# Modulation sums of a two-layer encoder moved from matmuls against c to elementwise work on GpSimd and VectorE

## The chip, the cores and the metric

The kernel runs on one core of a Trainium2 chip. The metric is device microseconds of one execution (median of several); lower is better. Engine names in the rows: PE is TensorE's matmul, PEld its weight load, DVE is VectorE, ACT is ScalarE, POOL is GpSimd, SP is the engine that issues most DMAs.

## What is computed

The reference runs DEPTH = 2 layers on x of 256 x 1024, everything in fp32:

```
c_act = silu(c)                                   # 1024 values
for l in range(2):
    mod = c_act @ w_ada[l] + b_ada[l]             # 1024 x 3072 matrix: shift, scale, gate
    shift, scale, gate = split(mod, 3)
    h = rms_norm(x, pre_norm_g[l]) * (1 + scale) + shift
    proj = h @ w_in[l]                            # 1024 x 4096
    att = dilated_attention(q, k, v, rel_bias) * silu(g_att)
    cnv = b_gate * short_conv(c_gate * u, conv_w[l]) * silu(g_conv)
    x = x + gate * rms_norm(concat(att, cnv) @ w_out[l], post_norm_g[l])
```

The change is about `c_act @ w_ada[l]`: a single row times 12 MB of weights for each layer. "Modulation sums" are these 3072 sums over 1024 inputs.

## The kernel before

All weights stream from HBM once, mostly in pieces of 1 MB (128 partitions x 8 KB) into six `raw` buffers of the pool `wp`. The main products are made in three passes of a split precision: each raw piece is split into a part `hi` (a cast on ScalarE, L145) and a part `lo` (raw minus hi on VectorE, L146), six buffers each, and `mm3` (L237 to L239) adds hi·hi, hi·lo and lo·hi.

The work has these stages, with the times of the profiled execution. A written-out prologue (to about 56 us) does layer 0's projections q, k, v and g row by row of w_in, together with the first two thirds of layer 0's modulation sums. Then comes layer 0's main stage (56 to 158 us): the remaining input projections in *chunks* of 256 columns (`chunk`, 48 matmuls each), the attention heads (`attend`), and three of the four steps of the output projection. After each chunk `side()` is called: it starts the heads and the side tasks listed for this step and lets each running side task go on to its next `yield`. A written-out transition (158 to 183 us) finishes the output projection, adds the residual, normalizes x again and makes layer 1's values. Layer 1's main stage (183 to 300 us) is like that of layer 0, and the output closes it. In the main stages the order on each engine is settled at compile time by a scheduler which takes the program's order as priority; each engine then runs its own list in order.

In the main stages the modulation sums are side tasks. Layer 0's stage has two gate tasks for its own gate and four `mods_task`s for layer 1's shift and scale (12 MB of w_ada in all), layer 1's has one gate task; each takes two pieces of 1024 x 256. Half of layer 1's gate is loaded at the end of layer 0 and summed in the transition (`add_sums(g_ps, gw, ...)`). A task yields twice and then emits its load and its sums. There are two ways to sum: `sums` has TensorE do it all, with silu(c) in 32 equal columns as the stationary operand (L295: 16 matmuls of 256 columns, four at a time in the four 32-row strips of the result); `vector_sums` multiplies and adds over the eight inputs of a partition on VectorE in two chains (L279, L281) and leaves four matmuls with a block of ones (L287). In layer 0 gate 0 and `mods_task(2)` go by `vector_sums`, the other four by `sums`; layer 1's gate task goes by `vector_sums`. An fp32 matmul shows as two instructions in the profile.

ScalarE copies each result from PSUM (L300). For shift and scale a GpSimd DMA packs it into a tile `parts`, which is transposed (L575) and finished by small VectorE operations in the transition (L578, L579, L268 to L270). For the gate, `gate_rows` adds two halves by a matmul with `pair` (L323), adds and multiplies b_ada and post_g on one row (L327, L328), writes the row to DRAM and reads it back to all partitions as `gg` (L330, L333).

Of the kernel before, what the change touches and what calls it, by code (L numbers as in the profile page):

```python
# [31 lines left out]
WC = 256  # L32
GATE_AT = ((0, 3), (None, 1))
ROWS_AT = (6, 5)
MODS_AT = (1, 2, 4, 5)
# [33 lines left out]
def encoder_kernel(ctx, tc, x, c, w_ada, b_ada, pre_g, w_in, conv_w, rel_bias, w_out, post_g, rows, out):  # L69
    nc = tc.nc  # L70
# [39 lines left out]
    ones = const.tile([P, 32], F32, name="ones")  # L110
# [86 lines left out]
    last_rstd = [None]  # L197
# [52 lines left out]
    def ada_load(l, k0, n):  # L250

        if n > 1:
            return [load_ada(l, base + k0 * P, n * P) for base in (0, D)]
        raw = wp.tile([P, 2, KC, n * P], F32, name="raw")
        for t in range(2):
            nc.sync.dma_start(raw[:, t], w_ada[l].rearrange("(k p) n -> p k n", p=P)[:, :, t * D + k0 * P:t * D + (k0 + n) * P])  # L256
        return [raw[:, t] for t in range(2)]

    def set_mods(l, k0, cols):

        n = cols.shape[-1]
        A, B = [m[:, k0:k0 + n] for m in mods[l]]
        if n == 1:
            shift, gain = vt[:, 8 + 24 * l + k0:9 + 24 * l + k0], vt[:, 56 + 8 * l + k0:57 + 8 * l + k0]
            nc.vector.tensor_scalar(A, cols[:, 1], scale1[:, l, k0:k0 + 1], gain, op0=ALU.add, op1=ALU.mult)
            nc.vector.tensor_scalar_add(B, cols[:, 0], shift)
            return
        nc.vector.tensor_add(A, cols[:, 1], scale1[:, l, k0:k0 + n])  # L268
        nc.vector.tensor_mul(A, A, vt[:, 56 + 8 * l + k0:56 + 8 * l + k0 + n])
        nc.vector.tensor_add(B, cols[:, 0], vt[:, 8 + 24 * l + k0:8 + 24 * l + k0 + n])  # L270

    def vector_sums(raws, pool, tag):

        for kk in range(KC // 2):
            for kh in range(2):
                k = kk + kh * (KC // 2)
                for raw in raws:
                    if kk == 0:
                        nc.vector.tensor_scalar_mul(raw[:, k], raw[:, k], c_rep[:, k, 0:1])  # L279
                    else:  # L280
                        nc.vector.scalar_tensor_tensor(raw[:, k], raw[:, k], c_rep[:, k, 0:1], raw[:, k - 1],  # L281
                                                       op0=ALU.mult, op1=ALU.add)
        g_ps = pool.tile([P, raws[0].shape[-1]], F32, name=tag)
        for kh in range(2):
            for t in range(2):
                j = 2 * kh + t
                nc.tensor.matmul(g_ps[32 * j:32 * j + 32, :], ones, raws[t][:, (kh + 1) * (KC // 2) - 1, :], start=True, stop=True)  # L287
        return take_sums(g_ps)
# [9 lines left out]
    def take_sums(g_ps, copy=nc.scalar.copy):  # L298
        acc = work.tile(list(g_ps.shape), F32, name="acc", bufs=5)
        copy(acc, g_ps)  # L300
        return acc
# [15 lines left out]
    gg = {}  # L317

    def gate_rows(l, accs):

        row_ps = pm.tile([2, 2, WC], F32, name="pm")
        for q in range(2):
            nc.tensor.matmul(row_ps[:, q], pair, accs[q], start=True, stop=True)  # L323
        b_row, g_row = [work.tile([2, 2, WC], F32, name=n, tag="junk", bufs=3) for n in ("b_row", "g_row")]
        nc.gpsimd.dma_start(b_row, b_ada[l, 2 * D:3 * D].rearrange("(h q n) -> h q n", h=2, q=2))
        nc.gpsimd.dma_start(g_row, post_g[l].rearrange("(h q n) -> h q n", h=2, q=2))
        nc.vector.tensor_add(b_row, row_ps, b_row)  # L327
        nc.vector.tensor_mul(b_row, b_row, g_row)  # L328
        r_dr = dram.tile([2, 2, WC], F32, name=f"r_dr{l}")
        nc.gpsimd.dma_start(r_dr, b_row)  # L330
        gg[l] = const.tile([P, 2, 512], F32, name="gg")
        src = r_dr[:]
        nc.gpsimd.dma_start(gg[l], bass.AP(tensor=src.tensor, offset=src.offset, ap=[[0, P], [1, D]]))  # L333

    def load_gate(l, q):
        return [load_ada(l, 2 * D + (q + 2 * h) * WC, WC) for h in range(2)]

    gate_acc = {}
# [34 lines left out]
    for l in range(DEPTH):  # L373
# [187 lines left out]

        if nxt:
            parts = const.tile([32, P], F32, name="parts")

        def mods_task(s):
            yield
            yield
            acc = (vector_sums if s == 2 else sums)(ada_load(l + 1, 2 * s, 2), pm, "pm")
            nc.gpsimd.dma_start(parts[8 * s:8 * s + 8], acc[0:P:32].rearrange("j (b p) -> j b p", p=P))
            if s < 3:  # L570
                return
            yield
            yield
            col_ps = pm.tile([P, 4, 2, 2, 2], F32, name="pm")
            nc.tensor.transpose(col_ps.rearrange("p s h t b -> p (s h t b)"), parts, ident[:32, :32])  # L575
            cols = small.tile([P, 2, KC], F32, name="cols", bufs=1)
            half = small.tile([P, 4, 2, 2], F32, name="half", bufs=1)
            nc.vector.tensor_copy(half, col_ps[:, :, 0])  # L578
            nc.vector.tensor_add(cols.rearrange("p t (s b) -> p s t b", b=2), col_ps[:, :, 1], half)  # L579
            set_mods(l + 1, 0, cols)  # L580

        def gate_task(q):
            yield
            yield
            gate_acc.setdefault(l, []).append((vector_sums if q == l else sums)(load_gate(l, q), pm, "pm"))

        def rows_task():
            with tc.issue_after(last_rstd[0].ins):
                gate_rows(l, gate_acc[l])
            yield  # L590
# [11 lines left out]
        for q, at in enumerate(GATE_AT[l]):  # L602
            if at is not None:
                starts[at].append(gate_task(q))
        starts[ROWS_AT[l]].append(rows_task())
        if nxt:
            for q, at in enumerate(MODS_AT):
                starts[at].append(mods_task(q))
# [99 lines left out]
        if nxt:  # L708
            vw_raw = [load_raw(l + 1, 2 * AW + i * WC) for i in range(2)]
            gw = load_gate(l + 1, 0)  # L710
# [46 lines left out]
        with tc.manual_schedule(engines=MANUAL):  # L757
# [40 lines left out]
            g_ps = pm.tile([P, WC], F32, name="pm")  # L798
            add_sums(g_ps, gw, range(2))
# [3 lines left out]
            add_sums(g_ps, gw, range(2, 4))  # L803
            gate_acc[l + 1] = [take_sums(g_ps)]
# [25 lines left out]
```

## Time and profile before

| | us |
|---|---|
| median of 3 runs | 310.91 (310.74 to 310.98) |
| profiled execution, its own time | 311.03 |
| its span (first to last instruction) | 309.3 |
| busy: PE, DVE, ACT, POOL | 300.4, 211.8, 178.1, 24.1 |

The span is what the views below cover; the profiled execution has 1.7 us around it. A matmul's row is as long as its passage through the array, and the next one starts before it ends, so a busy TensorE is judged by the distance of the starts. The granted TensorE clock is 1.00 of full speed in every stretch up to 300 us.

### The profile page before, as it was taken

Reading aid. Unit: us, or ns where it says so; the run is one execution under the profiler, and the core shown is the slowest. Engines: PE = TensorE matmul, PEld = TensorE weight load, DVE = VectorE, ACT = ScalarE, POOL = GpSimd, SP = SyncE. Lnnn points to the kernel's source line nnn. Section 1 sums busy time; section 2 is a strip of 40 time slices with the busy share of each in tenths; the row PEclk is TensorE's granted clock in tenths of the full one; section 3 lists DMA queues with packets and bytes.
Section 4 is the critical chain, followed back from the end, with each engine's and each line's share of the span. In section 5 each row is a group of like instructions: output and inputs, shape, how many; then the busy total and the mean of one; then the engine's idle time right before and its main releaser. Section 6 shows DMA issues by size and latency. Waiting matters only on the chain.

```text
span 309.3 us, 6050 instructions
## 1 busy us (share of the span) xinstructions
PE 300.4 (97%) x2421; PEld 261.3 (84%) x2421; DVE 211.8 (68%) x430; ACT 178.1 (58%) x318; POOL 24.1 (8%) x49
## 2 busy tenths in 40 slices
PE   8999999999999999999999999999999999999991
PEld 6878998899877779878677899999998989998881
DVE  3554446589988498688449798798868686845333
ACT  4633445599247243989437584569637695663211
POOL 5220000000000000110013410000000001000011
PEclk9999999999999999999999999999999999999998
DMA  7999999999979999989912399758548632000002
GB/s 244 327 350 330 322 351 343 358 350 348 313 248 344 348 348 323 404 281 351 345 65 66 114 350 344 227 153 242 152 135 272 265 137 70 0 2 0 2 35 102
DMA packets 65692, 72.39 MB, mean 234 GB/s; under 512 B 1778, under 2 KB 61526, under 8 KB 65664
## 3 DMA queue, kind: packets, MB, share of 16 engines
q1 hardware_dynamic: 64512, 70.39, 70.9%
q0 software_dynamic: 784, 1.20, 1.2%
q8 instruction: 19, 0.31, 0.4%
q10 hardware_dynamic: 368, 0.42, 0.4%
q14 instruction: 9, 0.07, 0.1%
HBM read 70.91 MB, written 1.07 MB: 233 GB/s over the span
## 4 chain that ended last, share of the span: by engine, by line
PE 83%; DVE 4%; SPq 4%; DMA 3%; POOL 1%; issue 1%; ACT 1%; POOLq 0%; DVEq 0%; ACTq 0%
PE pm L237 21%; PE pm L238 21%; PE pm L239 21%; PE ps L554 4%; DMA raw<-in_w_in 3%; PE pm L295 3%; PE ps L546 3%; SPq L394 2%; PE ps L295 2%; SPq L256 2%; PE ps L238 2%; PE ps L237 2%; PE ps L239 1%; PE ps L528 1%; PE ps L529 1%
## 5 line engine op out<-in xcount | busy, mean ns | idle before, releaser
L237 PE MATMUL pm<-hT_hi,hi 128*128 128x256 f32 x408 | 116.2, 285 | 0.0
L238 PE MATMUL pm<-hT_lo,hi 128*128 128x256 f32 x408 | 114.9, 282 | 0.1
L239 PE MATMUL pm<-hT_hi,lo 128*128 128x256 f32 x408 | 114.4, 280 | 0.0
L146 DVE TENSOR_TENSOR lo<-raw,hi 128x1024 fp32r<-128x1024 f32 (+1 forms) x94 | 94.0, 1028 | 29.6 <-ACT hi L145 29.2
L145 ACT CAST hi<-raw 128x1024 fp32r<-128x1024 f32 (+1 forms) x94 | 80.5, 893 | 32.9 <-PE pm L238 15.3
L237 PEld LDWEIGHTS pm<-hT_hi,hi 128*128 128x128 f32 x408 | 76.8, 188 | 5.6 <-issue 4.5
L238 PEld LDWEIGHTS pm<-hT_lo,hi 128*128 128x128 f32 x408 | 76.8, 188 | 2.5 <-issue 1.9
L239 PEld LDWEIGHTS pm<-hT_hi,lo 128*128 128x128 f32 x408 | 76.8, 188 | 1.2 <-issue 0.8
L237 PE MATMUL pm<-hi,hT_hi 128*128 128x512 f32 (+1 forms) x68 | 23.7, 348 | 0.0
L239 PE MATMUL pm<-hi,hT_lo 128*128 128x512 f32 (+1 forms) x68 | 23.6, 346 | 0.0
L238 PE MATMUL pm<-lo,hT_hi 128*128 128x512 f32 (+1 forms) x68 | 23.3, 343 | 0.0
L537 ACT ACTIVATE prob<-prob,mx 128x256 f32<-128x256 f32 x32 | 16.0, 503 | 4.0 <-DVE mx L534 3.9
L281 DVE SCALAR_TENSOR_TENSOR raw<-raw,c_rep 128x256 f32<-128x256 f32 x36 | 16.0, 477 | 0.1
L182 ACT ACTIVATE junk<-pm 128x512 f32<-128x512 f32 (+1 forms) x9 | 5.0, 550 | 17.2 <-PE pm L239 17.1
L239 PEld LDWEIGHTS pm<-hi,hT_lo 128*128 128x128 f32 x68 | 12.8, 188 | 2.2 <-DVE hT_lo L231 0.6
L237 PEld LDWEIGHTS pm<-hi,hT_hi 128*128 128x128 f32 x68 | 12.8, 188 | 2.0 <-DVE hT_hi L230 0.4
L724 DVE TENSOR_TENSOR og<-pm,gg 128x512 f32<-128x512 f32 (+1 forms) x9 | 5.6, 630 | 12.7 <-ACT junk L182 12.7
L238 PEld LDWEIGHTS pm<-lo,hT_hi 128*128 128x128 f32 x68 | 12.8, 188 | 1.3
L554 PE MATMUL ps<-pT,v_sb 128*64 128x256 f32 x64 | 13.8, 398 | 0.0
L238 PE MATMUL pm<-lo,mix_a 128*128 128x512 f32 (+1 forms) x36 | 13.4, 373 | 0.0
L237 PE MATMUL pm<-hi,mix_a 128*128 128x512 f32 (+1 forms) x36 | 13.4, 372 | 0.0
L239 PE MATMUL pm<-hi,mix_a 128*128 128x512 f32 (+1 forms) x36 | 12.7, 371 | 0.0
(176 smaller groups left out, 446.0 us busy)
## 6 DMA issues: line engine op xcount, KB each, us to landing
raw<-in_w_in SPq DMA_DIRECT2D x25, 1024.0 KB, 7.6
raw<-in_w_ada SPq DMA_DIRECT2D x16, 1024.0 KB, 10.8
raw<-in_w_ada SPq DMA_DIRECT2D x16, 512.0 KB, 8.4
raw<-in_w_out SPq DMA_DIRECT2D x8, 1024.0 KB, 6.9
raw<-in_w_in SPq DMA_DIRECT2D x7, 896.0 KB, 10.0
u<-t_dr SPq DMA_DIRECT2D x1, 1536.0 KB, 10.0
x_sb<-in_x SPq DMA_DIRECT2D x2, 512.0 KB, 4.3
gg<-r_dr POOLq DMA_DIRECT2D x2, 512.0 KB, 4.2
```

The costliest lines, as they stand in the source:

```text
L145: nc.scalar.copy(hi, raw)
L146: nc.vector.tensor_sub(lo, raw, hi.bitcast(F32))
L237: nc.tensor.matmul(o, ah, bh, start=first, stop=False, **kw)
L238: nc.tensor.matmul(o, ah, bl, start=False, stop=False, **kw)
L239: return nc.tensor.matmul(o, al, bh, start=False, stop=last, **kw)
L256: nc.sync.dma_start(raw[:, t], w_ada[l].rearrange("(k p) n -> p k n", p=P)[:, :, t * D + k0 * P:t * D + (k0 + n) * P])
L281: nc.vector.scalar_tensor_tensor(raw[:, k], raw[:, k], c_rep[:, k, 0:1], raw[:, k - 1], op0=ALU.mult, op1=ALU.add)
L295: nc.tensor.matmul(g_ps[32 * j:32 * j + 32, :], c_rep[:, kk + kh * (KC // 2), :], raws[t][:, kk + kh * (KC // 2), :], start=kk == 0, stop= ...
L394: row_dma[0] = nc.sync.dma_start(raw[:, a:b], w_in[0, k * P:(k + 1) * P, a:b])
L537: nc.scalar.activation(pr_sb[:, t, :], pr_sb[:, t, :], AF.Exp, scale=-1.0, bias=mx[:, t:t + 1], accum_out=sm[:, t:t + 1])
L546: turned[h] = nc.tensor.transpose(t_ps[:, kt, t * P:(t + 1) * P], pr_sb[:, t, kt * P:(kt + 1) * P], ident)
L554: taken[h] = nc.tensor.matmul(a_ps[(hh % 2) * HD:(hh % 2 + 1) * HD, :], qkv["v"][:, kt, hh * HD:(hh + 1) * HD], pT[hh][:, kt, :], start=kt ...
```

## The change

Every piece of 256 columns of w_ada in a main stage becomes a task of its own, given in `PIECES` by the step at which it starts, the engine and the number of yields: in layer 0 seven pieces on GpSimd ("P", four yields) and five on VectorE ("D", one yield), in layer 1 four on GpSimd. The engine multiplies by silu(c) and adds over the eight inputs of each partition: VectorE with one multiplication and seven chained multiply-adds, GpSimd with eight multiplications of 256 columns and three additions of 1024, 512 and 256 columns. After the yields TensorE adds over partitions: for a gate piece one matmul with a 128 x 128 block of ones, which leaves the sums in all partitions; for a shift or scale piece two matmuls whose moving operand is one column of ones. VectorE adds and multiplies the vectors straight from PSUM. `gate_tiles` loads b_ada and post_g broadcast to all partitions by two ScalarE-queue DMAs of 512 KB per layer. The sums in the transition, the `parts` tile, the copies on ScalarE and the trip of the gate through DRAM are gone; all of layer 1's gate is loaded in layer 1. The prologue's sums stay.

```diff
-GATE_AT = ((0, 3), (None, 1))
-ROWS_AT = (6, 5)
-MODS_AT = (1, 2, 4, 5)
+PIECES = (((0, "P", 4), (1, "P", 4), (1, "D", 1), (2, "P", 4),
+           (3, "D", 1), (4, "P", 4), (5, "P", 4), (5, "D", 1), (6, "P", 4), (7, "D", 1), (8, "P", 4), (9, "D", 1)),
+          ((0, "P", 4), (2, "P", 4), (4, "P", 4), (6, "P", 4)))
...
-    ones = const.tile([P, 32], F32, name="ones")
+    ones = const.tile([P, P], F32, name="ones")
...
-    def vector_sums(raws, pool, tag):
...
+    def scaled(raw, on):
+
+        if on == "D":
+            nc.vector.tensor_scalar_mul(raw[:, 0], raw[:, 0], c_rep[:, 0, 0:1])
+            for k in range(1, KC):
+                nc.vector.scalar_tensor_tensor(raw[:, k], raw[:, k], c_rep[:, k, 0:1], raw[:, k - 1],
+                                               op0=ALU.mult, op1=ALU.add)
+            return raw[:, KC - 1]
+        for k in range(KC):
+            nc.gpsimd.tensor_scalar(raw[:, k], raw[:, k], c_rep[:, k, 0:1], 1.0, op0=ALU.mult, op1=ALU.mult)
+        for n in (4, 2, 1):
+            nc.gpsimd.tensor_add(raw[:, 0:n], raw[:, 0:n], raw[:, n:2 * n])
+        return raw[:, 0]
...
-        acc = work.tile(list(g_ps.shape), F32, name="acc", bufs=5)
+        acc = work.tile(list(g_ps.shape), F32, name="acc", bufs=2)
...
-    def gate_rows(l, accs):
...
+    def gate_tiles(l):
+
+        gg[l] = const.tile([P, D], F32, name="gg")
+        gate_b[l] = const.tile([P, D], F32, name="gate_b")
+        for to, src in ((gg[l], post_g[l]), (gate_b[l], b_ada[l, 2 * D:3 * D])):
+            nc.scalar.dma_start(to, bass.AP(tensor=src.tensor, offset=src.offset, ap=[[0, P], [1, D]]))
+
+    def gate_piece(l, i, acc):
+
+        cs = slice(i * WC, (i + 1) * WC)
+        g_ps = pm.tile([P, WC], F32, name="pm")
+        nc.tensor.matmul(g_ps, ones, acc, start=True, stop=True)
+        nc.vector.tensor_add(gate_b[l][:, cs], g_ps, gate_b[l][:, cs])
+        nc.vector.tensor_mul(gg[l][:, cs], gg[l][:, cs], gate_b[l][:, cs])
+
+    def mods_piece(l, i, acc):
+
+        col_ps = pm.tile([P, 2], F32, name="pm")
+        for b in range(2):
+            nc.tensor.matmul(col_ps[:, b:b + 1], acc[:, b * P:(b + 1) * P], ones[:, 0:1], start=b == 0, stop=True,
+                             skip_group_check=True)
+        k0 = 2 * (i % 4)
+        ks = slice(k0, k0 + 2)
+        A, B = mods[l]
+        if i < 4:
+            nc.vector.tensor_add(B[:, ks], col_ps, vt[:, 8 + 24 * l + k0:10 + 24 * l + k0])
+        else:
+            nc.vector.tensor_add(A[:, ks], col_ps, scale1[:, l, ks])
+            nc.vector.tensor_mul(A[:, ks], A[:, ks], vt[:, 56 + 8 * l + k0:58 + 8 * l + k0])
...
-        def mods_task(s):
...
-        def gate_task(q):
...
-        def rows_task():
...
+        def piece_task(i, on, steps):
+            c0 = 2 * D + i * WC if i < 4 else (i - 4) * WC
+            acc = scaled(load_ada(l if i < 4 else l + 1, c0, WC), on)
+            for _ in range(steps):
+                yield
+            if i < 4:
+                gate_piece(l, i, acc)
+            else:
+                mods_piece(l + 1, i - 4, acc)
...
+        gate_tiles(l)
+        for i, (at, on, steps) in enumerate(PIECES[l]):
+            starts[at].append(piece_task(i, on, steps))
...
-            gw = load_gate(l + 1, 0)
...
-            g_ps = pm.tile([P, WC], F32, name="pm")
-            add_sums(g_ps, gw, range(2))
...
-            add_sums(g_ps, gw, range(2, 4))
-            gate_acc[l + 1] = [take_sums(g_ps)]
```

## Rows read from the trace of the kernel before

**Rows 1.** Page, first part: busy time, share of the span, instructions.

```profile
PE 300.4 (97%) x2421; PEld 261.3 (84%) x2421; DVE 211.8 (68%) x430; ACT 178.1 (58%) x318; POOL 24.1 (8%) x49
```

**Rows 2.** Windows by stage: us, busy us of PE, PEld, DVE, ACT, POOL; clock, DMA share, GB/s.

```profile
56.00:158.00 102.00, 102.00 (x807) 85.11 (x799) 77.79 (x159) 65.05 (x114) 3.85 (x6) 1.00 1.00 329
158.00:183.00 25.00, 24.34 (x172) 19.96 (x172) 20.90 (x41) 16.47 (x36) 8.60 (x14) 1.00 0.42 128
183.00:300.00 117.00, 117.00 (x898) 107.76 (x898) 81.65 (x146) 69.94 (x112) 2.15 (x5) 1.00 0.43 140
```

**Rows 3.** Timeline of PE in a plain chunk: start, us, line.

```profile
190.10 0.28 PE L239 MATMUL pm<-hT_hi,lo 128*128 128x256 f32 x1
190.22 0.28 PE L237 MATMUL pm<-hT_hi,hi 128*128 128x256 f32 x1
```

**Rows 4.** Waits of PE, the only one in the transition: us, times, longest.

```profile
PE ps L749 <- DVE xhat L786: 0.6, 1, 0.6
```

**Rows 5.** Chain by line, first 56 to 158 us, then 158 to 184 us.

```profile
by line: PE pm L237 22.7%; PE pm L239 21.3%; PE pm L238 21.0%; PE pm L295 9.4%; PE ps L554 6.2%; PE ps L546 4.0%; PE ps L238 2.7%; PE ps L237 2.7%; PE ps L239 2.7%; PE pm L287 2.2%; PE ps L528 2.1%; PE ps L529 1.9%; PE pm L323 0.8%; PE ps L
...
by line: PE pm L239 12.8%; PE pm L238 9.6%; PE pm L237 9.4%; issue 9.4%; DVE x_sb L729 8.5%; POOL rstd L213 8.1%; DVE hT_lo L231 6.5%; DVE junk L208 5.1%; DVE lo L146 4.7%; DVE og L724 4.6%; DVE vw_q_odd L146 4.4%; PE ps L749 4.1%; DVE hT_h
```

**Rows 6.** Chain in order of time: start, us on the chain, line.

```profile
102.44 1.85 PE pm L295 x28
...
234.78 0.57 PE pm L287 x8
...
250.51 0.95 PE pm L323 x4
```

**Rows 7.** Timeline of PE at a matmul of few columns.

```profile
57.03 0.28 PE L314 MATMUL ps<-pair,acc 128*128 128x2 f32 x2
57.17 0.36 PE L237 MATMUL pm<-hT_hi,hi 128*128 128x256 f32 x1
57.37 0.28 PE L238 MATMUL pm<-hT_lo,hi 128*128 128x256 f32 x1
```

**Rows 8.** Lines of DVE, 56 to 158 us: busy us, mean ns.

```profile
L146 DVE TENSOR_TENSOR lo<-raw,hi 128x1024 fp32r<-128x1024 f32 x26 | 31.1, 1221 | 4.1 <-ACT hi L145 4.1
L281 DVE SCALAR_TENSOR_TENSOR raw<-raw,c_rep 128x256 f32<-128x256 f32 x24 | 10.6, 478 | 0.1
...
L279 DVE TENSOR_SCALAR raw<-raw,c_rep 128x256 f32<-128x256 f32 x8 | 2.4, 348 | 0.0
...
L540 DVE RECIPROCAL rc<-sm 128x2 f32<-128x2 f32 x8 | 1.3, 163 | 2.3 <-ACT prob L537 2.2
...
L231 DVE TENSOR_TENSOR hT_lo<-h,hT_hi 128x256 fp32r<-128x256 f32 x1 | 0.4, 426 | 0.0
```

**Rows 9.** Timelines of POOL and DVE where the two engines meet.

```profile
160.06 0.57 POOL L194 TENSOR_TENSOR rstd<-me,neg_half 128x1 f32<-128x1 f32 x1
...
163.24 1.54 POOL L213 TENSOR_TENSOR rstd<-me,neg_half 128x1 f32<-128x1 f32 x1
...
163.15 1.23 DVE L146 TENSOR_TENSOR lo<-raw,hi 128x1024 fp32r<-128x1024 f32 x1
...
176.77 1.99 POOL L349 MEMSET k_low<- 64x1024 f32 x2 [0.66 <-PE ps L749]
...
177.21 0.67 DVE L230 CAST hT_hi<-h 128x256 fp32r<-128x256 f32 x1 [0.57 <-ACT h L226]
...
179.41 0.29 DVE L230 CAST hT_hi<-h 128x256 fp32r<-128x256 f32 x1
```

**Rows 10.** Lines of POOL by shape: busy us, mean ns.

```profile
L349 POOL MEMSET k_low<- 64x1024 f32 x4 | 3.8, 959 | 6.4 <-PE pm L387 5.6 <-PE ps L749 0.7
...
L86 POOL TENSOR_SCALAR_AFFINE_SELECT ident<-ident 128x128 f32<-128x128 f32 x1 | 0.3, 300 | 0.1
...
L191 POOL TENSOR_TENSOR me<-me,ms 128x1 f32<-128x1 f32 x1 | 0.2, 190 | 0.5 <-ACT junk L182 0.5
```

**Rows 11.** Timeline of SP's DMA issues: a pair of w_ada pieces, layer 0.

```profile
83.47 5.59 SPq L174 DMA_DIRECT2D raw<-in_w_ada  x2
```

More of the change, by code (lines that the diff above doesn't have):

```diff
@@ L250, in ada_load @@
     def ada_load(l, k0, n):
-        if n > 1:
-            return [load_ada(l, base + k0 * P, n * P) for base in (0, D)]
         raw = wp.tile([P, 2, KC, n * P], F32, name="raw")
@@ L259, in set_mods @@
     def set_mods(l, k0, cols):
[L261 to L268, printed above, removed]
@@ L269, in set_mods @@
-        nc.vector.tensor_mul(A, A, vt[:, 56 + 8 * l + k0:56 + 8 * l + k0 + n])
-        nc.vector.tensor_add(B, cols[:, 0], vt[:, 8 + 24 * l + k0:8 + 24 * l + k0 + n])
-    def vector_sums(raws, pool, tag):
[L274 to L288, printed above, removed]
+        A, B = [m[:, k0:k0 + 1] for m in mods[l]]
@@ new lines, in set_mods @@
+        shift, gain = vt[:, 8 + 24 * l + k0:9 + 24 * l + k0], vt[:, 56 + 8 * l + k0:57 + 8 * l + k0]
+        nc.vector.tensor_scalar(A, cols[:, 1], scale1[:, l, k0:k0 + 1], gain, op0=ALU.add, op1=ALU.mult)
+        nc.vector.tensor_scalar_add(B, cols[:, 0], shift)
+    def scaled(raw, on):
[10 more added lines that the diff above has]
+        return raw[:, 0]
@@ L315, in columns @@
         return col_ps
-    gg = {}
-    def gate_rows(l, accs):
[L321 to L333, printed above, removed]
@@ L335, in load_gate @@
-    def load_gate(l, q):
-        return [load_ada(l, 2 * D + (q + 2 * h) * WC, WC) for h in range(2)]
-    gate_acc = {}
+    gg, gate_b = {}, {}
+    def gate_tiles(l):
[9 more added lines that the diff above has]
+        nc.vector.tensor_mul(gg[l][:, cs], gg[l][:, cs], gate_b[l][:, cs])
@@ L558, in encoder_kernel @@
         nxt = l + 1 < DEPTH
-        if nxt:
-            parts = const.tile([32, P], F32, name="parts")
-        def mods_task(s):
[L566 to L580, printed above, removed]
-        def gate_task(q):
-            yield
-            yield
-            gate_acc.setdefault(l, []).append((vector_sums if q == l else sums)(load_gate(l, q), pm, "pm"))
-        def rows_task():
-            with tc.issue_after(last_rstd[0].ins):
-                gate_rows(l, gate_acc[l])
-            yield
+        def piece_task(i, on, steps):
[7 more added lines that the diff above has]
+                mods_piece(l + 1, i - 4, acc)
         o0 = 4 * AW
@@ L601, in encoder_kernel @@
         heads = [[h for h in range(NH) if HEAD_AT[l][h] == i] for i in range(16)]
[L602 to L608, printed above, removed]
+        gate_tiles(l)
+        for i, (at, on, steps) in enumerate(PIECES[l]):
+            starts[at].append(piece_task(i, on, steps))
         running = []
@@ L723, in gated @@
             half, at = cs.start // 512, slice(cs.start % 512, (cs.stop - 1) % 512 + 1)
-            nc.vector.tensor_mul(og[t][half][:, at], o_ps[t][n], gg[l][:, half, at])
+            nc.vector.tensor_mul(og[t][half][:, at], o_ps[t][n], gg[l][:, cs])
         def residual(t, cols=(0, 512, 1024)):
```

## The prediction

> **What bounds the kernel now.** I read the page first: TensorE is busy for 97% of the span [rows 1]. Since busy matmuls may still be slow ones, I then asked for the windows by stage [rows 2] and for the distance of the starts. Both main stages show TensorE busy from end to end, and in a plain chunk a matmul of 256 columns starts every 0.12 us [rows 3]; the list of waits names a single one on TensorE in the transition, 0.6 us [rows 4]. So in the main stages every matmul taken off shortens the stage, provided its feeders keep up. The chain by line says the same for 56 to 158 us: matmul lines and nothing else of weight. From 158 to 184 us it is mixed, with VectorE and GpSimd in front [rows 5]: the transition waits for the normalized x, not for TensorE.
>
> The reader should see two more things in [rows 2]. In layer 0's stage VectorE is busy for 77.8 of 102 us and the DMA engines all the time at 329 GB/s; in layer 1's stage they have 35 us and more than half of the time free. GpSimd is idle nearly throughout. If the change has a price, it is paid in layer 0.
>
> **TensorE's part.** The chain of layer 0's stage gives L295 9.4%, L287 2.2% and L323 0.8% of 102 us [rows 5]: 9.6 + 2.2 + 0.8 = 12.6 us, all removed. Added are four gate matmuls with a full block of ones: the chain has two full fp32 matmuls of 256 columns at L323 for 0.95 us [rows 6], so 0.48 each, 1.9 us. Eight shift and scale pieces make two matmuls of one column each. The nearest row is L314: its matmul takes 0.14 us to the next start, and the one behind it 0.20 in place of 0.12 [rows 7]; a pair costs 0.14 + 0.14 + 0.08 = 0.36, eight 2.9 us. Layer 0 saves 12.6 - 4.8 = 7.8 us. In layer 1, 0.57 + 0.95 go [rows 6] and four gate matmuls, 1.9, come: 0.4 us more.
>
> In the transition 32 instructions of sums go. They fill time in which TensorE waits for x anyway, and behind the second half it waits already [rows 4]: nothing. The small operations that finish shift and scale (five of about 0.17, by the 128x2 row of [rows 8]) leave VectorE, which is on this chain: at most 0.8, I take 0.4 us. TensorE's sum, if everything arrives in time: -7.8 + 0.4 - 0.4 = -7.8 us.
>
> **VectorE's part, layer 0.** The 32 operations of `vector_sums` go: 10.6 + 2.4 = 13.0 us busy [rows 8], and two row operations of about 0.7. A D piece is one L279 and seven L281 at the same means (2.4/8 and 10.6/24): 0.30 + 7 x 0.44 = 3.4 us, five 17.0. Four gate pieces add two operations of 256 columns (0.43 each by L231 [rows 8]): 3.4. Twelve narrow ones at 0.17: 2.0. Net 77.8 - 14.4 + 22.4 = 85.8 us, in a stage which TensorE would end after 102 - 7.8 = 94.2. That fits, with 8 us left. In layer 1 VectorE loses 7 and gains 3.4 us where 35 are idle: nothing.
>
> **GpSimd's part.** No row shows a wide multiplication on it. Its 128x128 select takes 0.30 and a one-column operation 0.19 us [rows 10]: 0.87 ns a column, so about 0.41 us for 256 columns. The memset of 64x1024, 0.96 us, has the same slope. An addition reads two operands: between the one-operand slope and twice that, the three together take 2.1 to 3.7 us. A piece: 8 x 0.41 + 2.1 to 3.7 = 5.4 to 7.0 us; of this 3.3 to 4.9 is streaming (1,792 + 2,048 columns, without the 0.19 that each of 11 instructions costs anyway). Seven pieces are 38 to 49 us of an engine that has about 98 free. A piece has four steps, some 30 us, before TensorE wants it.
>
> The trace speaks against this being free. A reciprocal root of one column takes 0.57 us, but 1.54 when it meets a `lo` subtraction on VectorE: it ends 0.40 us after the subtraction [rows 9]. In turn a cast on VectorE takes 0.67 in place of 0.29 us when GpSimd's memset runs [rows 9]. So each of the two engines can hold the other for an instruction. The Trainium skill, "SBUF — State Buffer", § Who interferes with whom, states it as an exclusive lock on a shared pair of ports, taken by VectorE operations with two SBUF inputs or in a two-port mode and by GpSimd, for the whole instruction; the rows agree as far as they go, and no row shows a wide GpSimd read holding a subtraction. By that rule alone, with whole instructions, the change would cost time: this is the first rival.
>
> What of VectorE is exposed? Of the 77.8 us the operations with two SBUF inputs, and the scalings and casts from SBUF, make 61 (thirteen rows of this view, from L146 with 31.1 to L231 with 0.4 [rows 8]). Less 13.0, plus 17.0, plus 2.4 of the added ones: 67 us by busy time; followed from start to start an L281 takes 0.40 and not 0.48 us, so 63 is nearer. Together with GpSimd: 63 + 23 to 34 (streaming only) = 86 to 97 us, or 63 + 38 to 49 (whole instructions) = 101 to 112. The delayed root ran 0.17 of its 0.57 us before it was held, and the delayed cast needed only a part of its 0.29 behind the memset, so an instruction's fixed part overlaps and the streaming time is the better price. I take its middle, 28: 91 us, just inside the 94.2, and allow 3 us for the places where a late VectorE operation stops TensorE in its fixed order (softmax scaling before the transposes above all). The lead of three chunks of `hi` and `lo` covers the rest.
>
> **Loads.** Before, a pair of pieces is issued at 83.5 [rows 11] and summed from 102.4 us [rows 6]: two buffers for about 22 us, six times. Now a P piece holds one for four steps of 8 us and the landing before them, about 40, seven times, a D piece about 18, five times: 370 against 264 buffer-us, one of the six buffers more on average. Traffic in the stage changes by -2 MB (layer 1's gate) - 0.5 + 1.0 MB. I price this at 0; it shows in a rival. ScalarE loses six copies and gains two DMA issues in this stage, and GpSimd's queue loses its small DMAs: nothing, ScalarE being busy for 65 of 102 us [rows 2].
>
> **Sum.** -7.8 + 3 = -4.8 us. The profiled execution took 311.0 us (span 309.3 and 1.7 around it), 0.1 above the median: I forecast 306 us.
>
> **Rivals.**
> - *The two engines hold each other for whole instructions.* Place: layer 0's stage. For it: [rows 9]; against: the fixed parts overlapped there, and layer 1 has room. It decides from the point at which 63 us and seven pieces exceed 102: 5.6 us per piece. At 7.0 the stage is 112 us and the kernel 10 us slower; in the middle of 5.6 and 7.0 it is 5, and TensorE's stops of 1 to 3 us add to either: 317 us. A page puts the additions at the upper end: the Trainium skill, "GPSIMD Engine Reference", § Performance versus the Vector engine, has 4,497 ns for an addition of 2,048 columns; an estimate from it is 3.9 us for the three, near the 3.7 above, and no run here shows it.
> - *No change.* The freed time is eaten by the stage's other limits: VectorE with GpSimd reaches 102 us, or the DMA engines, always busy now, deliver the stage's loads no faster. 310.5 us.
> - *TensorE waits for pieces or weights.* Its list is fixed; a piece that GpSimd finishes late, or a chunk which found no `raw` buffer, stops everything behind. For it: one buffer less where SP already waits for releases; against: 30 us of time for 7 us of work. One wait of about 1 us per P piece of layer 0 and one missed load of 5 us would turn -4.8 into +7: 313 to 318, I take 314 us.
>
> **Chances and range.** Forecast 0.52 (its own range 302.5 to 309.5: the lower end is the whole of TensorE's 7.8 us and half a microsecond more, the upper end VectorE's delays at twice what I allow), first rival 0.27, no change 0.12, late pieces 0.09. A difference of 0.2%, 0.6 us, is about what a measurement of this kernel can tell. Faster: 0.52 and a third of "no change", 0.56; same 0.08; slower 0.36. The range must take in most of the first rival: 303 to 319 us; about 0.05 lies below it and 0.12 above.
>
> **What would show it.** Right: L295 gone after 60 us; layer 0's stage about 97 us long; GpSimd rows of 0.4 us for 256 columns and under 2 us for 1,024; no wait of TensorE above 1 us in the main stages. `lo` subtractions longer than 1.22 us with GpSimd rows beside them, and waits of TensorE for VectorE, show the first rival; waits for `raw` of GpSimd or for casts, the last. The prediction fails if a GpSimd piece takes over 6 us of VectorE's way, or if TensorE's new matmuls cost more than 0.5 us each.

## The result and the profile after

The changed kernel takes 333.21 us (median of 4 runs, 332.32 to 335.02) against 310.83 (310.55 to 310.98) before: a ratio of 1.0729, interval 1.0683 to 1.0774, 22.4 us slower. The forecast was 306, its range 303 to 319. The profiled execution took 332.32 us, its span is 330.6. The stages below are read from the two profiled executions, whose spans differ by 21.3 us.

Page of the kernel after, first part, and the windows by stage (columns as in [rows 2]):

```profile
PE 299.9 (91%) x2276; PEld 267.6 (81%) x2276; DVE 247.8 (75%) x441; ACT 175.6 (53%) x310; POOL 144.1 (44%) x158
```

```profile
65.05:178.72 113.67, 96.87 (x654) 85.40 (x653) 106.44 (x177) 59.24 (x101) 76.38 (x77) 0.92 0.76 243
178.72:204.00 25.28, 23.12 (x140) 19.52 (x139) 20.34 (x36) 16.56 (x35) 8.22 (x13) 1.00 0.78 252
204.00:321.00 117.00, 116.63 (x893) 108.36 (x892) 84.63 (x132) 69.45 (x111) 51.08 (x47) 1.00 0.45 145
```

I cut both kernels at the same events (the ScalarE activation that ends the prologue, the first square of the output projection, the last transposes of the transition). The prologue went from 61.6 to 65.0 us, layer 0's main stage from 95.9 to 113.7, the transition from 18.1 to 18.0, the rest from 133.7 to 133.9. So the whole loss lies in layer 0's stage (17.8) and the prologue (3.4). The stage before, by the same events:

```profile
61.62:157.56 95.94, 95.94 (x761) 79.87 (x761) 74.52 (x151) 60.60 (x106) 3.85 (x6) 1.00 1.00 329
```

TensorE has 145 instructions fewer on the page, yet its busy time is the same as in [rows 1]; VectorE has 36 us more. In layer 0's stage VectorE is busy for 106 of 114 us and the granted TensorE clock is 0.92. Layer 1's stage holds 51 us of GpSimd work and is not longer: VectorE, busy for 85 of 117 us, has room there.

The chain by line of 65 to 179 us, and TensorE's longest waits in the whole execution (the second is in the prologue):

```profile
by line: DVE lo L148 23.0%; DVE raw L271 13.9%; DMA raw<-in_w_in 11.5%; DVE prob L541 8.5%; issue 7.9%; DVE y L609 4.7%; ACT hi L147 4.6%; DVE raw L269 2.8%; DVE prob L533 2.4%; DVE pT L547 1.6%; ACT k_hh L368 1.5%; DVE gg L322 1.4%; DVE hT
```

```profile
PE pm L241 <- DVE lo L148: 9.5, 3, 6.4
PE ps L285 <- DMA raw<-in_w_ada: 3.3, 2, 2.7
PE ps L545 <- DVE prob L541: 3.0, 4, 2.1
PE pm L239 <- ACT hi L147: 2.3, 2, 1.6
```

In [rows 5] this chain was TensorE's; now VectorE leads it. Its lines in the same stretch, and GpSimd's:

```profile
L148 DVE TENSOR_TENSOR lo<-raw,hi 128x1024 fp32r<-128x1024 f32 x26 | 34.7, 1357 | 5.4 <-ACT hi L147 5.4
L271 DVE SCALAR_TENSOR_TENSOR raw<-raw,c_rep 128x256 f32<-128x256 f32 x35 | 23.5, 673 | 0.4
L541 DVE TENSOR_SCALAR prob<-prob,rc 128x256 f32<-128x256 f32 x16 | 11.1, 735 | 0.0
L533 DVE CUSTOM_DVE_ANT_0 prob<-ps,u 128x256 f32<-128x256 f32 x16 | 6.1, 416 | 0.1
```

```profile
L275 POOL TENSOR_SCALAR raw<-raw,c_rep 128x256 f32<-128x256 f32 x56 | 42.5, 776 | 63.6 <-DMA raw<-in_w_ada 43.0 <-DVE pT L547 13.1 <-PE pm L240 7.5
L277 POOL TENSOR_TENSOR raw<-raw 128x1024 f32<-128x1024 f32 x7 | 18.8, 2685 | 0.4
L277 POOL TENSOR_TENSOR raw<-raw 128x512 f32<-128x512 f32 x7 | 10.1, 1439 | 0.5
L277 POOL TENSOR_TENSOR raw<-raw 128x256 f32<-128x256 f32 x7 | 5.3, 757 | 0.4
```

The same VectorE instructions took 1,221 and 478 ns before [rows 8]. The kernel before's softmax scaling, and its operation that is L533 after:

```profile
L542 DVE TENSOR_SCALAR prob<-prob,rc 128x256 f32<-128x256 f32 x16 | 4.9, 347 | 0.1
L534 DVE CUSTOM_DVE_ANT_0 prob<-ps,u 128x256 f32<-128x256 f32 x16 | 6.1, 420 | 0.3
```

The operations that became longer take their inputs from SBUF; L533, one of whose inputs is in PSUM, keeps its time. One stop in full, from the timelines of VectorE, GpSimd and TensorE:

```profile
81.85 4.84 DVE L271 SCALAR_TENSOR_TENSOR raw<-raw,c_rep 128x256 f32<-128x256 f32 x3
...
87.84 1.41 DVE L148 TENSOR_TENSOR lo<-raw,hi 128x1024 fp32r<-128x1024 f32 x1
...
81.75 4.65 POOL L277 TENSOR_TENSOR raw<-raw 128x256 f32<-128x256 f32 x3
...
82.66 0.28 PE L240 MATMUL pm<-hT_lo,hi 128*128 128x256 f32 x1
89.30 0.58 PE L241 MATMUL pm<-hT_hi,lo 128*128 128x256 f32 x1 [6.37 <-DVE lo L148]
89.68 0.42 PE L239 MATMUL pm<-hT_hi,hi 128*128 128x256 f32 x1
89.90 0.42 PE L240 MATMUL pm<-hT_lo,hi 128*128 128x256 f32 x1
90.11 0.41 PE L241 MATMUL pm<-hT_hi,lo 128*128 128x256 f32 x1
```

Three VectorE steps of a D piece, 0.48 us each when alone, take 4.84 us beside three GpSimd additions (the shape shown is the first one's). The second of each, by itself:

```profile
82.47 2.53 POOL L277 TENSOR_TENSOR raw<-raw 128x1024 f32<-128x1024 f32 x1
...
82.84 2.45 DVE L271 SCALAR_TENSOR_TENSOR raw<-raw,c_rep 128x256 f32<-128x256 f32 x1
```

The addition ends at 85.00 and the VectorE step at 85.29 us. The other two steps also end 0.28 us behind the addition that they met. So VectorE was held to the end of each of these GpSimd instructions. The `lo` behind them comes late and TensorE stands for 6.4 us. Then its matmuls start every 0.21 us in place of the 0.12 of [rows 3]. The windows of two us (columns as in [rows 2]) show why:

```profile
82.00:84.00 2.00, 0.93 (x9) 0.73 (x7) 1.96 (x2) 0.18 (x1) 2.00 (x2) 1.00 0.92 294
84.00:86.00 2.00, 0.00 (x0) 0.00 (x0) 1.97 (x2) 0.00 (x0) 1.92 (x2) 1.00 0.10 32
86.00:88.00 2.00, 0.00 (x0) 0.00 (x0) 1.97 (x7) 0.81 (x3) 2.00 (x4) 0.94 0.00 0
88.00:90.00 2.00, 0.70 (x3) 0.70 (x4) 2.00 (x3) 2.00 (x4) 2.00 (x3) 0.50 0.00 0
90.00:92.00 2.00, 2.00 (x11) 2.00 (x11) 2.00 (x5) 0.16 (x1) 2.00 (x3) 0.50 0.04 8
92.00:94.00 2.00, 2.00 (x12) 2.00 (x11) 2.00 (x3) 0.00 (x0) 2.00 (x4) 0.50 0.64 183
94.00:96.00 2.00, 2.00 (x17) 2.00 (x17) 2.00 (x2) 0.00 (x0) 2.00 (x1) 0.86 0.99 341
```

After the idle stretch the granted clock is 0.50, the lower of the two levels (1.2 of 2.4 GHz), and returns to 1.00 some five us after TensorE resumed. So this stop is paid twice. The DMA engines stand still as well (share 0.00 from 86 to 90 us): no load was issued between 76.9 and 91.5 us, while SyncE's queue waited for VectorE.

### The profile page after: what moved, and what is told of

It reads as the page before. It is cut to its first block, busy times and chain, and to the rows that moved or that the text cites. A ratio compares the mean times of both kernels' runs of the same rounds, so it can differ in the third digit from the quotient of the medians.

```text
span 330.6 us, 5878 instructions
## 1 busy us (share of the span) xinstructions
PE 299.9 (91%) x2276; PEld 267.6 (81%) x2276; DVE 247.8 (75%) x441; ACT 175.6 (53%) x310; POOL 144.1 (44%) x158
## 4 chain that ended last, share of the span: by engine, by line
PE 53%; DVE 26%; DMA 7%; ACT 6%; issue 4%; POOL 1%; SPq 0%; DVEq 0%; ACTq 0%; POOLq 0%
PE pm L239 14%; PE pm L241 13%; PE pm L240 13%; DVE lo L148 8%; DVE raw L271 5%; DMA raw<-in_w_in 4%; DVE prob L541 3%; DMA raw<-in_w_ada 3%; PE ps L285 3%; ACT hi L147 2%; PE ps L553 2%; DVE y L609 2%; PE ps L545 1%; DVE x_sb L702 1%; DVE raw L269 1%
## 5 line engine op out<-in xcount | busy, mean ns | idle before, releaser
L241 PE MATMUL pm<-hT_hi,lo 128*128 128x256 f32 x408 | 117.6, 288 | 9.5 <-DVE lo L148 9.5
L148 DVE TENSOR_TENSOR lo<-raw,hi 128x1024 fp32r<-128x1024 f32 (+1 forms) x94 | 103.3, 1126 | 25.1 <-ACT hi L147 24.8
L239 PE MATMUL pm<-hT_hi,hi 128*128 128x256 f32 x408 | 118.9, 291 | 2.3 <-ACT hi L147 2.3
L275 POOL TENSOR_SCALAR raw<-raw,c_rep 128x256 f32<-128x256 f32 x88 | 69.5, 807 | 73.4 <-DMA raw<-in_w_ada 46.4
L241 PEld LDWEIGHTS pm<-hT_hi,lo 128*128 128x128 f32 x408 | 79.3, 194 | 12.1 <-DVE lo L148 10.9
L239 PEld LDWEIGHTS pm<-hT_hi,hi 128*128 128x128 f32 x408 | 79.5, 195 | 4.3 <-ACT hi L147 2.7
L277 POOL TENSOR_TENSOR raw<-raw 128x1024 f32<-128x1024 f32 (+2 forms) x33 | 58.0, 1759 | 2.2
L271 DVE SCALAR_TENSOR_TENSOR raw<-raw,c_rep 128x256 f32<-128x256 f32 x35 | 23.5, 673 | 0.4
L541 DVE TENSOR_SCALAR prob<-prob,rc 128x256 f32<-128x256 f32 x32 | 19.2, 640 | 0.2
L545 PE MATMUL ps<-ident,prob 128*128 128x128 f32 x64 | 11.5, 283 | 3.0 <-DVE prob L541 3.0
```

The costliest lines, as they stand in the source:

```text
L148: nc.vector.tensor_sub(lo, raw, hi.bitcast(F32))
L239: nc.tensor.matmul(o, ah, bh, start=first, stop=False, **kw)
L241: return nc.tensor.matmul(o, al, bh, start=False, stop=last, **kw)
L275: nc.gpsimd.tensor_scalar(raw[:, k], raw[:, k], c_rep[:, k, 0:1], 1.0, op0=ALU.mult, op1=ALU.mult)
L277: nc.gpsimd.tensor_add(raw[:, 0:n], raw[:, 0:n], raw[:, n:2 * n])
L541: nc.vector.tensor_scalar_mul(pr_sb[:, t, :], pr_sb[:, t, :], rc[:, t:t + 1])
```

## The experiments

Theories: (A) GpSimd and VectorE hold each other, the prediction's first rival; (B) pieces hold `raw` buffers and loads come late; (C) VectorE's own share of the sums is too much; (D) the early broadcasts cost. In the table "end" is the end of layer 0's main stage on the trace; DVE and POOL are their busy us from 62 us to that end, from one window each (in after, e2, e3 and e14 it takes in the end of a longer prologue).

| kernel | us | ratio (interval) | end | DVE | POOL |
|---|---|---|---|---|---|
| before | 310.8 | | 157.6 | 74.5 | 3.9 |
| after | 333.2 | 1.0729 (1.0683, 1.0774) | 178.7 | 109.2 | 76.4 |
| e1_late_tiles | 332.0 | 1.0681 (1.0650, 1.0712) | 178.1 | 106.3 | 69.5 |
| e2_all_dve | 335.0 | 1.0777 (1.0709, 1.0845) | 179.8 | 103.4 | 0 |
| e3_ghost | 328.7 | 1.0574 (1.0500, 1.0648) | 173.9 | 84.9 | 15.0 |
| e4_free | 309.9 | 1.0001 (0.9943, 1.0060) | 156.9 | 65.6 | 0 |
| e5_free_short | 304.3 | 0.9781 (0.9750, 0.9811) | 151.2 | 66.0 | 0 |
| e6_only_d | 316.9 | 1.0186 (1.0156, 1.0215) | 163.7 | 80.9 | 0 |
| e7_only_p | 319.7 | 1.0277 (1.0247, 1.0307) | 166.0 | 78.1 | 68.7 |
| e8_ghost_main | 317.75 | 1.0213 (1.0184, 1.0243) | 164.2 | 93.8 | 78.3 |
| e9_d_short | 310.6 | 0.9985 (0.9964, 1.0007) | 157.1 | 79.7 | 0 |
| e10_full_two | 334.6 | 1.0761 (1.0697, 1.0825) | 180.2 | 104.0 | 73.6 |
| e11_ghost_mult | 311.4 | 1.0010 (0.9997, 1.0022) | 158.1 | 79.5 | 44.4 |
| e12_mix_v | 318.1 | 1.0229 (1.0176, 1.0282) | 163.9 | 80.5 | 3.5 |
| e13_ghost_add | 312.6 | 1.0068 (1.0031, 1.0104) | 159.0 | 85.1 | 38.3 |
| e14_ghost_add_narrow | 320.0 | 1.0291 (1.0261, 1.0321) | 166.1 | 79.7 | 24.0 |
| e15_ghost_mult_wide | 311.1 | 1.0001 (0.9989, 1.0012) | 157.6 | 79.2 | 30.7 |
| e16_full_narrow | 326.65 | 1.0506 (1.0451, 1.0561) | 174.4 | 102.6 | 81.3 |
| e17_ghost_add_narrow2 | 311.8 | 1.0043 (1.0013, 1.0073) | 158.2 | 83.3 | 53.3 |
| e18_full_mult | 316.1 | 1.0168 (1.0139, 1.0198) | 163.2 | 85.3 | 38.7 |

Any edit can make the program order TensorE's and VectorE's lists anew. Compared instruction by instruction, the lists of these two engines are the same in e1, e6, e16 and e18, and in e4 and e7; in e8, e11, e13, e15 and e17 they are before's, but for two instructions of VectorE's and, in e8, four of TensorE's. Inside such a set the times compare GpSimd's work (in e4 and e7 only that) and nothing else; between sets, and so in e4 against e5 or e6, in e5 against e9 and in after against e1, a new order is mixed in.

**e1: broadcasts later.** The kernel after, with layer 0's `gate_tiles` issued behind the prologue's last activation (all of e4 to e7, e9, e10, e16, e18 build on it).

```diff
-            nc.scalar.activation(warm, hT_lo[:, KC - 1, 0:1].bitcast(F32), AF.Exp, scale=0.0)
+            main = nc.scalar.activation(warm, hT_lo[:, KC - 1, 0:1].bitcast(F32), AF.Exp, scale=0.0)
+            with tc.issue_after(main.ins):
+                gate_tiles(0)
```

> The changed kernel, with layer 0's two broadcast loads issued on ScalarE's queue behind the last instruction of the prologue instead of at 1.8 and 4.4 us. Theory 'the broadcasts delay the first weights': the prologue's end comes back from 60.8 to about 57.4 us and the kernel takes about 330 us (333.2 less 3.4). Rival 'the late start is chance or has another cause': prologue still at 60.8 us, 333 us.

The prologue, 61.6 us before and 65.0 after by the cut used here, is back at 61.3 us, and TensorE's wait for the first weights falls from 3.3 to 0.3 us. But the end of the stage moves by 0.7 only. D is real in its place and worth 1.2 us of 22, with a new order mixed in.

**e2: no GpSimd.** All twelve pieces of layer 0 are `"D", 1`.

> The changed kernel with all twelve pieces of layer 0 on VectorE (one yield), layer 1 as it is. Theory 'GpSimd and VectorE hold each other': lo subtractions of layer 0 back to 1.22 us, VectorE then carries 12 x 3.4 us of pieces, about 105 busy us in the stage, which takes about 106 us instead of 118: 321 us in all. Rival 'pieces hold the raw buffers too long': pieces are held for one step instead of four, the stage falls to what TensorE needs, 95 to 98 us: 311 to 314 us, and VectorE is not the limit. If neither: 333.

Both theories missed. VectorE's multiply-adds keep their unheld time (L271 477 ns), but it has 84 multiply-adds, 38 us, in place of 35 and is busy for 103 us, nearly as long as in after, by its own work. Moving GpSimd's pieces to VectorE is no cure.

**e3: GpSimd's work beside the kernel before.** Seven pieces on a scratch tile that nobody reads.

```diff
+        for k in range(KC):
+            part = scratch[:, (k % 3) * WC:(k % 3 + 1) * WC]
+            nc.gpsimd.tensor_scalar(part, part, c_rep[:, k, 0:1], 1.0, op0=ALU.mult, op1=ALU.mult)
+        for n in (960, 512, 256):
+            nc.gpsimd.tensor_add(scratch[:, 0:n], scratch[:, 0:n], scratch[:, 0:n])
```

> The kernel before, with the GpSimd instructions of seven pieces (8 multiplications of 256 columns and additions of 960, 512 and 256) added in layer 0's stage at the same steps on a scratch tile that nothing else reads; VectorE, TensorE, loads and buffers have the work of before. Theory 'GpSimd and VectorE hold each other': lo subtractions stretch beyond 1.22 us beside GpSimd rows and the kernel takes 320 to 329 us. Rival 'buffers and order': nothing else waits for the scratch tile, 310 to 312 us.

Nothing tied the work to its stage and it ran early: GpSimd is busy for 70 us of a prologue that grew to 73.9, and 12.3 of the 17.7 us lost are there. It says that work without a reader costs, not what it costs in layer 0's stage.

**e4, e5: no work over inputs at all; short holds.**

```diff
     def scaled(raw, on):
+        return raw[:, 0]
```
```diff
-(0, "P", 4), (1, "P", 4), (1, "D", 1), ...
+(0, "P", 1), (1, "P", 1), (1, "D", 1), ...
```

> The kernel of the run with late broadcasts, without any multiplication or addition over inputs (TensorE adds the first eighth of each piece over partitions, so the sums are left out): what TensorE's side of the change would give if the rest were free. By the prediction's term: 7.8 us less than before, 303 us. If TensorE's saving was mis-sized or the loads bind: 307 to 311 us.

> As e4_free (no multiplication or addition over inputs is done, so the sums are left out), with every GpSimd piece's buffer given back one step after its start in place of four. Theory 'the pieces hold the raw buffers': TensorE's saving of 7.8 us comes out, 302 to 304 us, and the waits for loads in the prologue and the main stage shrink. Rival 'TensorE's new small matmuls cost what the old ones cost, so there was no saving': stays at 309 to 311 us.

Together they speak for B, at some 5 us. With buffers held for four steps nothing is gained (ratio 1.0001; e4's six runs lie between 309.5 and 313.6 us); given back after one, 6.5 us are. The order of the lists differs too, so the hold's share of the 5.6 us between them is not shown by itself. The chain by line of the stage (first e4, then e5) shows loads in front of TensorE in e4:

```profile
by line: DMA raw<-in_w_in 33.0%; PE pm L240 13.6%; PE pm L241 12.4%; PE pm L239 11.9%; DMA raw<-in_w_out 5.2%; ACT hi L147 4.4%; PE ps L557 4.3%; DVE lo L148 3.9%; PE ps L549 2.5%; PE ps L241 2.2%; PE pm L330 2.2%; PE ps L240 1.8%; PE ps L2
```

```profile
by line: PE pm L239 19.3%; PE pm L241 18.9%; PE pm L240 18.9%; DMA raw<-in_w_in 16.3%; PE ps L557 6.6%; PE ps L549 3.7%; PE pm L330 2.9%; issue 2.8%; ACT prob L540 2.2%; PE ps L531 2.1%; ACT hi L147 2.1%; POOL rstd L215 1.6%; PE ps L532 1.5
```

**e6, e7, e9: one engine's pieces alone.** The other engine's are left as in e4 (e9: as in e5).

> As e4_free, but the five VectorE pieces of layer 0 do their multiplications and additions; the GpSimd pieces still load and are summed over partitions, without the work over inputs (so most sums are left out). Theory 'GpSimd and VectorE hold each other': VectorE alone has room, 310 to 313 us, an STT of 256 columns stays at 480 ns. Rival 'VectorE's load alone is too much': 318 us or more.

> As e4_free, but the GpSimd pieces do their work and the five VectorE pieces are left out. VectorE then has 17 us less than with all pieces. Theory 'GpSimd and VectorE hold each other': still 318 us or more, lo subtractions and scalings of the softmax stretched. Rival 'the cost is VectorE's load and GpSimd only adds a little': 310 to 313 us.

> As e6_only_d (five VectorE pieces do their work, the GpSimd pieces do none, so most sums are left out), but the GpSimd pieces' buffers are given back after one step in place of four, as in e5_free_short (304.3 us). Theory 'VectorE's pieces cost only because buffers were short': 304 to 307 us. Rival 'their 20 us on VectorE cost 7 us of the stage by themselves': 311 us.

VectorE's five pieces cost 7.0 us over e4, between the two expectations, and 6.3 over e5. So with short holds too they cost about as much, which speaks for C and not for B; both steps have a new order mixed in. GpSimd's seven alone cost 9.8 over e4 in the same order (A), and with VectorE's pieces present 15.1 (e6 to e1, in the same order): beside VectorE's pieces they cost more than by themselves.

**e8, e11, e13, e15, e17: unread GpSimd work in layer 0's stage.** The kernel before, with e3's piece held in place by a small copy of a chunk's result: whole (e8), multiplications alone (e11), additions alone (e13), multiplications in instructions of 928, 928 and 192 (e15), additions in instructions of 160 to 256 (e17). e14 was meant as e17, but four of its seven additions per piece did not depend on the copy and ran in the prologue, which grew by 5.0 us; it tells nothing of its question.

```diff
+    def ghost_piece(i):
+        for k in range(KC):
+            part = scratch[:, (k % 3) * WC:(k % 3 + 1) * WC]
+            nc.gpsimd.tensor_scalar(part, part, tick[:, i:i + 1], 1.0, op0=ALU.mult, op1=ALU.mult)
+        for n in (928, 512, 256):
+            nc.gpsimd.tensor_add(scratch[:, 0:n], scratch[:, 0:n], scratch[:, 0:n])
...
+                nc.scalar.copy(tick[:, step[0]:step[0] + 1], o[:, 0, 0:1])
```

> The kernel before, with seven GpSimd pieces (eight multiplications of 256 columns, additions of 928, 512 and 256) on a scratch tile whose results nobody reads, one behind the chunk of steps 0, 1, 2, 4, 5, 6, 7 of layer 0. No buffer, load or matmul changes. VectorE is busy for 78 of 102 us there. Theory 'the two engines hold each other for whole instructions': layer 0's stage grows by 8 us or more (318 to 325 us), with VectorE's rows stretched. Rival 'GpSimd is harmless, buffers and late pieces cost': 310 to 312 us.

> As e8_ghost_main (317.75 us), but the unread GpSimd pieces make only their eight multiplications of 256 columns, not the three additions. Cost in proportion to GpSimd's busy time, 43 of 75 us: 315 us. If only the additions, with two operands, hold VectorE: 311 to 312 us. If the multiplications alone do: 317 to 318 us.

> As e8_ghost_main (317.75 us), but the unread GpSimd pieces make only the additions of 928, 512 and 256 columns (and a multiplication of one column that starts them). If additions hold VectorE by themselves: 316 to 318 us. If only the sum of both exceeds what VectorE has left: 311 to 313 us.

> As e13_ghost_add, the same 1,696 columns of additions per piece in seven instructions of 160 to 256 columns. If the two operands cost: as e13. If the length of one instruction does: 311 to 313 us, with e13 at 314 us or more.

> As e11_ghost_mult (311.4 us), the same 2,048 columns of multiplication per piece in instructions of 928, 928 and 192. If the length of one instruction costs: 314 us or more. If multiplications, with one operand, are harmless: 311 to 312 us.

> As e13_ghost_add (additions alone, unread, in layer 0's stage: 312.6 us), with the same columns in instructions of 160 to 256, all held back to the stage by three multiplications of one column. If the length of one instruction is what holds VectorE: 311 to 312 us. If the two operands do, whatever the length: 312.5 us or more.

Here no load, `raw` buffer or matmul differs (only `acc` has two buffers in place of five, and e15, which has that too, takes before's time), so A is shown: e8 costs 6.8 us. Read DVE against POOL. The multiplications add about 41 and 27 us to GpSimd and 5 to VectorE in either form, and the time does not move; the additions add 34 us to GpSimd and 10.6 to VectorE (1.7 us of time); all of it adds 19 to VectorE, and that is beyond what the stage could hide. So, as far as these runs go, there is a step in the cost: VectorE may grow by 5 to 10 us for under 2 us of time, by 19 for 7. Short additions (e17) lengthen VectorE by little less, 8.7 us. Their time, 311.8, lies where the expectation put short instructions that hold less, but it can't be told from e13's 312.6: the two intervals overlap. VectorE's busy time decides.

**e16, e18: the additions of the changed kernel, short, or left out.**

```diff
         for n in (4, 2, 1):
-            nc.gpsimd.tensor_add(raw[:, 0:n], raw[:, 0:n], raw[:, n:2 * n])
+            for k in range(n):
+                nc.gpsimd.tensor_add(raw[:, k], raw[:, k], raw[:, n + k])
```

> As e1_late_tiles (all work done, 332.0 us), with every GpSimd addition split into instructions of 256 columns (seven per piece in place of three). If the length of one instruction sets what VectorE loses: 325 us or less. If GpSimd's and VectorE's summed time does: 332 to 337 us, the extra fixed parts being on GpSimd.

> As e1_late_tiles (332.0 us) without GpSimd's three additions per piece (so the sums of its pieces are incomplete); 316.9 us is the time without its multiplications too (e6). If the additions carry the loss: 317 to 321 us. If cost goes by GpSimd's busy time: 323 to 325 us. If the multiplications carry it: 328 us or more.

Without its additions GpSimd costs nothing: e18 stands at e6's time. VectorE's lines in layer 0's stage, first e18, then e1:

```profile
L148 DVE TENSOR_TENSOR lo<-raw,hi 128x1024 fp32r<-128x1024 f32 x26 | 31.8, 1236 | 7.7 <-ACT hi L147 7.5
L271 DVE SCALAR_TENSOR_TENSOR raw<-raw,c_rep 128x256 f32<-128x256 f32 x35 | 17.7, 504 | 0.3
```

```profile
L148 DVE TENSOR_TENSOR lo<-raw,hi 128x1024 fp32r<-128x1024 f32 x26 | 36.2, 1409 | 5.1 <-ACT hi L147 4.8
L271 DVE SCALAR_TENSOR_TENSOR raw<-raw,c_rep 128x256 f32<-128x256 f32 x35 | 26.1, 746 | 0.3
```

In e18 the multiplications themselves are held (711 ns in the mean; the shortest of after take 471), and VectorE hardly; with additions it is VectorE that waits. Short additions give back 5.3 us of the 15.9 and land between their two expectations. The timelines show where the two kinds differ. A multiplication, too, is waited for to its end, as here in e11:

```profile
80.60 0.64 POOL L348 TENSOR_SCALAR scratch<-scratch,tick 128x256 f32<-128x256 f32 x1
...
80.82 0.69 DVE L281 SCALAR_TENSOR_TENSOR raw<-raw,c_rep 128x256 f32<-128x256 f32 x1
```

VectorE ends 0.27 us behind it, but is only 0.2 us late, because the multiplication is short. An addition of 256 columns makes such a step 0.4 to 0.5 us late (0.95 us in after, 0.48 alone), one of 1,024 columns 2.0 (the stop above).

**e10, e12: two versions.** e10 is e1 with GpSimd's pieces taken after two steps; e12 is the kernel before with one more pair by `vector_sums` (`s in (1, 2)`).

> As e1_late_tiles (all work done, 332.0 us), but TensorE takes a GpSimd piece two steps after its start in place of four. If held buffers were a cost of their own also beside the work (5.6 us between e4_free and e5_free_short): 327 to 329 us. If the engines' common time sets the stage: 331 to 334 us, with longer waits of TensorE for GpSimd's sums.

> The kernel before, with one more pair of layer 1's modulation pieces (the second) multiplied and added on VectorE in place of TensorE, and nothing on GpSimd. TensorE loses 16 matmuls that run four abreast, 2.2 to 2.4 us, VectorE gains 6.7 us on 78 of 102. If VectorE still had room: 308.6 to 309.2 us. If its further load costs as much as TensorE gains: 311 us; if more: 312 to 314 us.

e10 is no faster: nothing of the 5.6 us between e4 and e5 comes out here. e12, outside all its expectations, takes 7.1 us more with 5.9 us more on VectorE. TensorE saved nothing there: L295's busy time in the stage falls from 10.2 to 8.5 us and that of L287, four matmuls a pair, grows from 2.9 to 5.6. Its waits in the stage make 2.7 us more, and its list is in another order; the rest of the cause stays open. No version here beats the kernel before with all sums done.

## Why the prediction was wrong

The sum, rebuilt from the runs: before 310.8; TensorE's saving to e5, -6.5; longer holds, +5.6 (e4); VectorE's pieces, +7.0 (e6); GpSimd's multiplications, -0.8, which is no difference (e18); its additions, +15.9 (e1); early broadcasts, +1.2 (after): 333.2. Only GpSimd's two terms compare runs with the same lists; the others have a new order mixed in.

- *TensorE's part*, -7.8 forecast: right within two microseconds (e5's stage is 6.0 us shorter, the kernel 6.5; the freed VectorE time and the short holds are in it as well). The eight pairs, forecast at 2.9, are L330's 2.9% of a chain of 96 us. The transition and layer 1 moved by 0.2 us at most.
- *VectorE's part*, "That fits, with 8 us left": wrong. The busy time came as forecast, 81 us in e6 where 85.8 stood for a longer window, but five pieces at 84% busy already cost 6.3 us (e9). TensorE's order is fixed and each feeder has its place in VectorE's list, so a piece ahead of a `lo` or a scaling delays TensorE even where VectorE idles later. That is argued from after's stop at 82.7 us and from e6's and e9's time; which of e9's waits make the 6.3 us was not separated.
- *GpSimd's part*: the step that failed. The hold itself was sized nearly right: "streaming time", 28 us; VectorE grew by 25.4 from e6 to e1 (80.9 to 106.3). But the text added it to the 63 us of VectorE's work that can conflict and compared 91 with TensorE's 94.2. VectorE must do all of its work in order: 85.8 + 28 = 114, far past 94. The bound on VectorE's own list was never formed; by the prediction's own terms it excludes 306. The runs put 15.1 us on this step (e6 to e1), where the forecast allowed 3 for all of VectorE's delays. That 114 is also the length of after's stage is luck: the 85.8 stand for a longer window, and VectorE is idle for 7 us of that stage. In part the 28 is luck as well: GpSimd was busy for 69 to 76 us where 38 to 49 were forecast (the three additions take 4.9 us, not 2.1 to 3.7), and not every instruction met VectorE.
- *Whole instructions or streaming?* Both engines wait for whole instructions, as the first rival had it, and the fixed part overlaps, as the prediction said: a VectorE step is late by the GpSimd instruction that it meets, less 0.2 to 0.6 us in the rows above. The Trainium skill, "SBUF — State Buffer", § Who interferes with whom, says that VectorE operations with two SBUF inputs contend with any GpSimd instruction that reads SBUF and that the order of issue decides who blocks; the traces agree that both sides are held, and L533, which reads PSUM, is not. What the prediction did not have is how unlike the two kinds are: multiplications cost VectorE 4 us in 39 of GpSimd (e6 to e18), additions 21 in 34 (e18 to e1). An estimate from single rows is near for the additions: one of each length makes VectorE 0.4 + 0.9 + 2.0 us late, 23 us for seven pieces. For 56 multiplications at 0.2 it is at most 11; fewer than half of that came.
- *Loads*, priced at 0: up to 5.6 us when nothing else is late (e4 against e5, a new order included). The estimate of one buffer more on average was on the page; "SP already waits for releases" should have priced it.
- *3 us for late VectorE work*: TensorE stands idle for 16.8 us of the stage (113.67 less 96.87), e5 for 2.1 (89.95 less 87.81); and for the same work in another order it is busy 9.1 us longer. 14.7 + 9.1 = 23.7, before rounding, is the stage's difference to e5. Of the second term the half clock makes about 6 us, an estimate: TensorE is busy for 13.6 us of the stage's 17.1 at 0.50, where a matmul starts every 0.21 us in place of 0.12. The other 3 us stay open. This term was in no case of the prediction.
- *The rivals.* The first had the place, the sign, the engines and the whole instructions, but its price was 16 us short: it too counted 63 in place of 85.8, and no clock. The third, late pieces, was wrong in its subject: TensorE hardly waited for GpSimd's sums, it waited for `lo` (10.9 us of the 16.8), scalings and `hi`; in e1, with another order, for `hi` and scalings (8.0 and 7.8 of 20.8).
- *Unforeseen*: the broadcasts of 512 KB were issued at 1.8 and 4.4 us, between the first weights, and TensorE waited 3.3 us for the weights behind them (the L285 row; 0.2 before, 0.3 in e1).

What stays open: why so few of the multiplications hold VectorE, which of VectorE's delays make TensorE's stops, and how much of each step between differently ordered lists is the order.

## What to carry to other kernels

Before moving work to GpSimd, add the time that VectorE will be held to everything that VectorE does in that stage, and compare this with the stage; conflicting work alone is not the measure. A stage at 78% of VectorE with TensorE in fixed order has little room: with the lists kept, 5 us more cost nothing, 19 cost 7 (e12, with new lists, paid 7.1 for 5.9). And a stop of TensorE can cost more than its length: behind the one of 6.4 us the clock was at half for some five us more.

## What the runs showed of the hardware

GpSimd's multiplication of 256 columns by a column takes 0.47 us unheld, 0.65 to 0.78 in the mean beside a busy VectorE; its two-operand addition of 1,024 columns 2.5 to 2.7 us. A VectorE step of 256 columns with two SBUF inputs that was held by either ended 0.27 to 0.29 us behind it. A microsecond of such multiplication lengthened VectorE by 0.11 to 0.12 us, one of addition by 0.3 to 0.6 (e11, e18; e13, e1). An operation from PSUM (L533, 416 ns) was never lengthened.
